# Seven products for one more down projection, keys and values kept in device memory, and waits by tile

## The chip, the cores and the metric

The kernel runs on one core of one Trainium2 chip. The core has five engines that work side by side, each through its own list of instructions in order: TensorE (PE in the profile, its weight loads PEld), VectorE (DVE), ScalarE (ACT), GpSimd (POOL) and SyncE (SP, which here only issues DMAs). DMAs are issued from the lists of SP, ACT and POOL and run on 16 DMA engines. The metric is the time of one execution on the device in microseconds (us), as the median of several runs; lower is better.

## What is computed

The reference is one step of a small two-layer decoder over 520 tokens: a prompt of 512 and 8 sample sequences with one token each. Every layer is half a SwiGLU feed-forward, a mixer, and another half feed-forward. Layer 0 mixes by causal pooling, layer 1 by sliding-window attention (window 128, 16 heads, 4 key/value heads) with keys and values that are projected once between the layers.

```python
def _swiglu(x, wg, wu, wd):
    return (jax.nn.silu(x @ wg) * (x @ wu)) @ wd      # D_MODEL 1024, D_FF 2816

for l in range(2):
    if l == 1:
        kv = _rmsnorm(x, kv_norm_g) @ w_kv            # shared keys (rotated) and values
        ...
    x = x + 0.5 * _swiglu(_rmsnorm(x, norm_g[l, 0]), w_gate[l, 0], w_up[l, 0], w_down[l, 0])
    x = x + (pool mixer of layer 0, or attention of layer 1)(_rmsnorm(x, norm_g[l, 1]))
    x = x + 0.5 * _swiglu(_rmsnorm(x, norm_g[l, 2]), w_gate[l, 1], w_up[l, 1], w_down[l, 1])
y = _rmsnorm(x, final_norm_g)
```

Beside `y` the step returns the last pooling inputs and the last window of keys and values, all in float32. There are four half feed-forwards ("half layers" 0 to 3); the change is about number 2, the first of layer 1.

## The kernel before

All activations stand transposed in on-chip memory: `x` is 8 tiles of 128 features by 520 tokens. Each float32 operand is split into a high and a low part that the matmul takes at full rate (`split`, line 315: ACT makes the high part, L319 and L322; DVE the low one, L320 and L323). A product of two operands is then three matmuls (`terms`: high by high, and the two mixed ones). A matmul has a weight block of 128x128 as the stationary operand and 260 tokens, half of the 520, as the moving one.

**Weights.** `Weights` (line 127) loads weights in chunks of 1 MB into three `raw` buffers (SP queue, L334), and splits them piece by piece into `wh` (ACT, L260) and `wl` (DVE, L261), up to five pieces ahead of PE (line 330). PE takes pieces in order with `W.get`.

**Feed-forward.** `ffn` (line 794) goes through the 22 hidden tiles of D_FF in three parts of 8, 8 and 6 (`PARTS`). In each part it makes the hidden tiles (gate, up, silu, product) and then adds the part's down projection onto `x`. The first `NPL` tiles of a half layer are plain (`mm`, L535), the others use Strassen's seven products in Winograd's form (`strassen_tile`, line 684; `product`, L563): weights and tokens are cut into 2 by 2 blocks, and 7 block products take the place of 8. The weights' sums are made by two accumulating DMAs from the POOL queue (L191, L192) and two DVE additions (L197, L201), the tokens' sums by DVE.

**Down projection.** It is plain too, save for the parts in `SEVEN` (line 33): the middle part of half layers 0, 1 and 3. There `HiddenSums` (line 586) makes the blocks and sums of the hidden tiles while they are produced, in the tiles `ph` and `pl` among others, and `strassen_down` (line 718) makes two of the eight output tiles at a time from 7 products. The plain one makes an output tile from 8 hidden tiles times 3 matmuls times 2 token halves and adds it to `x` (L823, L824).

**Keys and values.** Between half layers 1 and 2 the keys `kT` and the values `vtok` are made and stay in a pool `kvp` of their own until attention: `outputs` (line 1216) turns them and writes the window outputs from the POOL queue, `attention_prep` (line 1242) runs during the last down projection of half layer 2; it loads the old keys `kc` (L1247), puts the new ones into their first row (L1248) and splits `kT` and `vtok` into the operands of attention (`tl`). In attention every third softmax tile `sm` takes the place of `kT` in `kvp` (line 1363), the other two are in the pool `at`.

**What sets the order.** The kernel is traced into a scheduler that gives each engine its order of instructions by simulated times; what is marked with `later` or `seq` stays in the order of the program. The steps of attention follow the hand-written `PLAN` (line 60) and so does PE there. Memory comes from pools that are opened and closed one after another over the same addresses; as written, the first tile of a pool waits for the users of the pool that had its bytes.

Of the kernel before, what the change touches and what calls it, by code (L numbers as in the profile page):

```python
# [29 lines left out]

FIRST = 264
NPL = (4, 3, 2, 3)
SEVEN = {(0, 1), (1, 1), (3, 1)}
HD = 64
NB = SP // P
WINS = (2, 4, 8, 16)
# [244 lines left out]
def yoco_step(ctx, tc, ins, outs):  # L281
# [43 lines left out]
    def later(ins):  # L325

        return tc.keep_in_program_order(ins)
# [527 lines left out]
                by_parts(hs)  # L855

    def ff_pool():
        return tc.tile_pool(name="ff", bufs=2)

    def deferred(n, tmp, tag, tags, lst, w=TOK, hold=False):  # L860

# [166 lines left out]
        after = deferred(1, tmp, "g", XX, mov1, TW, True)  # L1028
        ffn(0, tmp, mov0, start_hooks(tmp, 0, tt, 2), tt, HH, after, pool_prep(), first, hold=True)

    with tc.tile_pool(name="pm", bufs=2) as pm:
        for k in range(KT):
            split(tuple(z[:, TOK:TW] for z in mov1[k]), sts[:, k, :])

# [109 lines left out]
        ffn(1, tmp, mov2, start_hooks(tmp, 2, tt, 2), tt, HH, deferred(N_KV, tmp, "g", XX, movk))  # L1144


    kvs = ExitStack()
    kvp = kvs.enter_context(tc.tile_pool(name="kvp", bufs=1))
    kT2 = kvp.tile([P, 2, TOK], F32, tag="kT", name="kT")
    kT = [kT2[:, g, :] for g in range(2)]  # L1150
    vtok = kvp.tile([P, NB, 256], F32, name="vtok")
    knew = kvp.tile([NS, 256], F32, name="knew")
    vnew = kvp.tile([NS, 256], F32, name="vnew")
    swap = [i + 8 if i < 8 else i - 8 if i < 16 else i for i in range(32)]

    def rope(out, banks, cosr, sinr, pool, tags):
# [11 lines left out]
    with ff_pool() as tmp:  # L1168

        s4 = sinks.rearrange("p (g i b e) -> p g i b e", g=2, i=4, b=4)  # L1170
        sr = sraw.rearrange("p (g e i) -> p g i e", g=2, e=2)
        for b in range(4):
            for g in range(2):
                V.tensor_copy(s4[:, g, :, b, :], sr[:, g])
        V.tensor_scalar(nsinks, sinks, -1.0, None, op0=ALU.mult)
        V.tensor_scalar(sink_s[:, 1:2], sink_s[:, 0:1], -1.0, None, op0=ALU.mult)
        cs = rawp.tile([P, 2, TOK], F32, tag="raw", name="cs")
        nc.scalar.dma_start(cs.rearrange("p a t -> p (a t)"), consts[:, C_COS : C_COS + 2 * TOK])

        def kv_pass(after):  # L1180
            banks = [duo() for _ in range(2)]
            for k0 in (0, 4):
                ws = [W.get(), W.get()]
                W.prefetch()
                for k in range(k0, k0 + 4):
                    for w, bk in zip(ws, banks):
                        mm(w, k - k0, movk[k], bk, k == 0, k == KT - 1)
                    after(k)
            return banks

        def during_k(k):
            if k == 1:
                rstd_tok()
            if k == 3:
                rstd_all()

        mov3, tt = [], {}
        steps = sums(tmp, 3, tt)

        def during_v(k):  # L1200
            mov3.append(pair(HH, [P, TOK]))
            split(mov3[k], x[k], gcol(3, k))
            if k >= 4:
                next(steps)

        kb = kv_pass(during_k)
        for i in range(2):
            V.tensor_tensor(cs[:, i, :], cs[:, i, :], R, op=ALU.mult)
        for g in range(2):
            rope(kT[g], kb[g], cs[:, 0, :], cs[:, 1, :], tmp, ("g", "t"))  # L1210
        vb = kv_pass(during_v)
        vT = [tmp.tile([P, TOK], F32, tag="g", name="vT") for g in range(2)]
        for g in range(2):
            V.tensor_tensor(halves(vT[g]), vb[g][:, :, :H], halves(R), op=ALU.mult)

        def outputs():
            win = tmp.tile([P, 256], F32, tag="t", name="win")
            pk = ps()
            for g in range(2):
                T.transpose(pk[:, g * P : (g + 1) * P], kT[g][:, 384:512], ident)  # L1220
                T.transpose(pk[:NS, 256 + g * P : 256 + (g + 1) * P], kT[g][:, SP:], ident)
            S.copy(win, pk[:, :256])
            S.copy(knew, pk[:NS, 256:512])
            nc.gpsimd.dma_start(k_win_p[0].rearrange("s g d -> s (g d)"), win)
            nc.gpsimd.dma_start(k_win_s[:, 127].rearrange("b g d -> b (g d)"), knew)
            for b2 in range(2):
                pv = ps()
                for b in (2 * b2, 2 * b2 + 1):
                    for g in range(2):
                        o = (b % 2) * 256 + g * P  # L1230
                        T.transpose(pv[:, o : o + P], vT[g][:, b * P : (b + 1) * P], ident)
                S.copy(vtok[:, 2 * b2 : 2 * b2 + 2, :], pv.rearrange("p (b c) -> p b c", b=2))  # L1232
            nc.gpsimd.dma_start(v_win_p[0].rearrange("s g d -> s (g d)"), vtok[:, 3, :])
            pvs = ps()
            for g in range(2):
                T.transpose(pvs[:NS, g * P : (g + 1) * P], vT[g][:, SP:], ident)
            S.copy(vnew, pvs[:NS, :256])
            nc.gpsimd.dma_start(v_win_s[:, 127].rearrange("b g d -> b (g d)"), vnew)

        kc, kk, vv = [], [], []  # L1240

        def attention_prep():


            for i in range(4):
                kc.append(splp.tile([P, 2, 256], F32, tag="S", name="kc", bufs=4))
                later(nc.sync.dma_start(kc[i], cache_k[2 * i : 2 * i + 2].rearrange("b s g d -> s b (g d)")))  # L1247
                nc.gpsimd.dma_start(kc[i][0:1], knew[2 * i : 2 * i + 2, :])  # L1248
            yield
            for i in range(4):  # L1250
                z = pair(("tl", "tl"), [P, SP])
                if i < 2:
                    kk.append(z)
                    split(z, kT[i][:, :SP])
                else:
                    vv.append(tuple(a.rearrange("p (b c) -> p b c", b=2) for a in z))
                    split(vv[-1], vtok[:, 2 * i - 4 : 2 * i - 2, :])
                if i:
                    yield
            for i in range(4):  # L1260
                pk = ps()
                for j in range(4):
                    T.transpose(pk[:, j * P : (j + 1) * P], kc[i][:, j // 2, (j % 2) * P : (j % 2 + 1) * P], ident)
                S.copy(kc[i].rearrange("p b c -> p (b c)"), pk)
                yield

        step = lambda: next(steps, None)
        hooks = [step, outputs] + [step] * 4
        ffn(2, tmp, mov3, hooks, tt, XX, deferred(4, tmp, "g", HH, mov4), attention_prep())


    mov5, mov6 = [], []
    with tc.tile_pool(name="at", bufs=2) as at:
        cst = at.tile([P, 512], F32, name="cst", bufs=1)
        nc.scalar.dma_start(cst, consts[:, C_MASK : C_MASK + 512])
        csq = at.tile([P, 2, TOK], F32, name="csq", bufs=1)
# [59 lines left out]
        class Unit:  # L1336
# [22 lines left out]
            def softmax(self):  # L1359

                c0 = self.t * 8 + self.h * 4
                nm, self.den = (at.tile([P, 4], F32, tag=n, name=n) for n in ("nm", "den"))
                pool = at if (2 * self.t + self.h) % 3 < 2 else kvp
                sm = pool.tile([P, 2, TOK], F32, tag="sm" if pool is at else "kT", name="sm")
                sm = sm.rearrange("p b (e c) -> p (b e) c", e=2)
                seq(V.tensor_copy(sm[:, :, 256], nsinks[:, c0 : c0 + 4]))
                self.sms = []
                for i in range(4):
                    bi, e = i // 2, i % 2
                    b = self.bs[bi]  # L1370
                    n = 256 if b else P
                    mk = C_MASK + 256 if b else C_MASK
                    self.sms.append(sm[:, i, 256 - n :])
                    seq(
                        V.tensor_tensor_reduce(  # L1375
                            out=sm[:, i, 256 - n : 256],
                            in0=self.pe[e][:, bi * 256 : bi * 256 + n],
                            in1=cst[:, mk : mk + n],
                            op0=ALU.add,
                            op1=ALU.min,  # L1380
                            scale=nr8[:, b : b + 1],
                            scalar=nsinks[:, c0 + i : c0 + i + 1],
                            accum_out=nm[:, i : i + 1],
                        )
                    )
                for i in range(4):
                    z = sm[:, i, 256 - (256 if self.bs[i // 2] else P) : 257]
                    seq(
                        S.activation(
                            z, z, AF.Exp, scale=-1.0, bias=nm[:, i : i + 1], accum_out=self.den[:, i : i + 1]  # L1390
                        )
                    )
# [179 lines left out]
        def load_values():  # L1572
            vc.append(rawp.tile([P, NS, 256], F32, tag="raw", name="vc"))
            later(nc.sync.dma_start(vc[0], cache_v.rearrange("b s g d -> s b (g d)")))
            nc.gpsimd.dma_start(vc[0][0:1], vnew)

        def w_load(n):
            W.load(o_chunk + n)
# [35 lines left out]
        after_o = deferred(5, at, "rp0", XX, mov6)  # L1614
        for m in range(KT):
            o_part(m, 4, after=after_o)

    kvs.close()

    with ff_pool() as tmp:  # L1620
        tt = {}
# [239 lines left out]
```

## Time and profile before

| | us |
|---|---|
| median of 3 runs (lowest, highest) | 1674.66 (1671.61, 1676.63) |
| the profiled execution, its own time | 1678.03 |
| its span, first to last instruction | 1676.2 |
| what lies around the span | 1.83 |

The profile has one execution. A busy share is the time in which an engine works, over the span. The views used below are the page with its chain of waits (which engine the end of the program hung on, followed backwards), the busy time of every engine in chosen stretches, the list of waits of an engine, the groups of instructions, and the timeline. In a row of the stretches stand the length, then for each engine the busy time and the number of instructions, the granted clock of TensorE, the busy share of the DMA engines and GB/s. In a timeline row stand start, duration, engine, line, operation, output<-inputs, and in brackets the idle time before it with what ended it. The mean granted clock of the run is 0.991.

### The profile page before, as it was taken

To read this page: it belongs to the slowest core of one execution; us is meant where nothing else is said; L and a number is where in the kernel's file an instruction comes from. 1 tells how busy PE (TensorE), PEld (TensorE's weight loads), DVE (VectorE), ACT (ScalarE), POOL (GpSimd) and SP (SyncE) were. 2 spreads that over 40 slices of the span, in tenths; PEclk is the share of its full clock that TensorE was granted. 3 is DMA by queue.
4 is the path that set the end of the run, shared out by engine and by line. 5 is a ranking of instruction groups with operands and counts; after the bars stand their busy time and mean duration, and the time that the engine had idled before them with its cause. 6 is when DMAs were issued, how large, how long until landed. Compare 5 with 4: busy or idle time off the path is not lost.

```text
span 1676.2 us, 34643 instructions
## 1 busy us (share of the span) xinstructions
PE 1644.5 (98%) x13626; PEld 1632.1 (97%) x13626; DVE 1307.3 (78%) x2532; ACT 920.7 (55%) x1867; POOL 187.0 (11%) x248
## 2 busy tenths in 40 slices
PE   9999999999999999999999999999889999999997
PEld 9999999999999999999999999999889999999997
DVE  6866999887875999888775875886776785799876
ACT  5743655665652664655552642655775663465555
POOL 0101111000101111101101101101210100111100
PEclk9999999999999999999999999999979999999999
DMA  8545778753555778645645855644122545577851
GB/s 223 132 133 125 174 184 177 187 167 88 110 151 127 178 170 198 149 130 133 148 143 127 173 147 127 155 140 105 42 51 76 133 114 156 130 180 174 178 134 52
DMA packets 337199, 235.42 MB, mean 140 GB/s; under 512 B 10878, under 2 KB 309606, under 8 KB 336996
## 3 DMA queue, kind: packets, MB, share of 16 engines
q1 hardware_dynamic: 306814, 181.00, 38.4%
q0 software_dynamic: 26464, 47.12, 17.6%
q10 hardware_dynamic: 3758, 5.09, 1.0%
q8 instruction: 107, 1.75, 0.4%
q14 instruction: 56, 0.46, 0.1%
HBM read 183.45 MB, written 5.04 MB: 112 GB/s over the span
## 4 chain that ended last, share of the span: by engine, by line
PE 89%; DVE 5%; DMA 2%; ACT 2%; issue 2%; POOL 0%; ACTq 0%; DVEq 0%; POOLq 0%
PE ps L563 50%; PE ps L535 33%; DMA S<-raw 1%; DVE wl L261 1%; PE ps L1445 1%; PE ps L1077 1%; DMA pr<-in_bands_dram 0%; DVE sm L1375 0%; PE ps L1052 0%; PE ps L1538 0%; PE ps L1735 0%; DVE xl L320 0%; PE ps L1414 0%; ACT wh L260 0%; PE ps L1357 0%
## 5 line engine op out<-in xcount | busy, mean ns | idle before, releaser
L260 ACT ACTIVATE wh<-raw 128x512 fp32r<-128x512 f32 (+1 forms) x754 | 449.4, 620 | 425.8 <-PE ps L535 232.1
L261 DVE TENSOR_TENSOR wl<-raw,wh 128x512 fp32r<-128x512 f32 (+1 forms) x754 | 495.1, 675 | 153.1 <-ACT wh L260 150.6
L563 PE MATMUL ps<-th,wh 128*128 128x260 f32 x1216 | 344.0, 283 | 1.7 <-ACT sa L701 0.9
L563 PE MATMUL ps<-tl,wh 128*128 128x260 f32 x1216 | 342.4, 282 | 0.0
L563 PE MATMUL ps<-th,wl 128*128 128x260 f32 x1216 | 341.0, 282 | 0.2 <-DVE wl L261 0.2
L563 PEld LDWEIGHTS ps<-th,wh 128*128 128x128 f32 x1216 | 228.5, 188 | 3.6 <-ACT sa L701 1.4
L563 PEld LDWEIGHTS ps<-tl,wh 128*128 128x128 f32 x1216 | 229.0, 188 | 0.0
L563 PEld LDWEIGHTS ps<-th,wl 128*128 128x128 f32 x1216 | 227.9, 188 | 0.4 <-DVE wl L261 0.4
L192 POOL DMA_DIRECT2D raw<-raw x88 | 75.8, 862 | 1177.2 <-DVE wl L261 452.3
L563 PE MATMUL ps<-xh,wh 128*128 128x260 f32 x720 | 203.1, 283 | 0.7 <-ACT sb L698 0.7
L563 PE MATMUL ps<-xl,wh 128*128 128x260 f32 x720 | 202.3, 282 | 0.0
L563 PE MATMUL ps<-xh,wl 128*128 128x260 f32 x720 | 200.9, 282 | 0.0
L535 PE MATMUL ps<-hh,wh 128*128 128x260 f32 x956 | 193.7, 284 | 0.6 <-ACT vtok L1232 0.6
L535 PE MATMUL ps<-hl,wh 128*128 128x260 f32 x956 | 193.4, 283 | 0.0
L535 PE MATMUL ps<-hh,wl 128*128 128x260 f32 x956 | 192.3, 283 | 0.0
L535 PE MATMUL ps<-xl,wh 128*128 128x260 f32 x736 | 149.7, 284 | 0.3 <-DVE xl L951 0.3
L535 PE MATMUL ps<-xh,wh 128*128 128x260 f32 x736 | 149.0, 285 | 0.0
L535 PEld LDWEIGHTS ps<-hh,wh 128*128 128x128 f32 x956 | 147.1, 189 | 1.5 <-ACT vtok L1232 0.9
L535 PE MATMUL ps<-xh,wl 128*128 128x260 f32 x736 | 148.0, 283 | 0.0
L535 PEld LDWEIGHTS ps<-hl,wh 128*128 128x128 f32 x956 | 147.9, 189 | 0.0
L535 PEld LDWEIGHTS ps<-hh,wl 128*128 128x128 f32 x956 | 147.6, 189 | 0.0
L563 PEld LDWEIGHTS ps<-xh,wh 128*128 128x128 f32 x720 | 135.4, 188 | 1.3 <-ACT sb L698 1.3
(325 smaller groups left out, 3369.6 us busy)
## 6 DMA issues: line engine op xcount, KB each, us to landing
raw<-in_ffn_w_gate_dram SPq DMA_DIRECT2D x87, 512.0 KB, 4.2
raw<-in_ffn_w_up_dram SPq DMA_DIRECT2D x87, 512.0 KB, 6.5
raw<-raw POOLq DMA_DIRECT2D x88, 256.0 KB, 3.4
S<-raw POOLq DMA_DIRECT2D x88, 256.0 KB, 4.5
raw<-in_ffn_w_down_dram SPq DMA_DIRECT2D x20, 1024.0 KB, 4.9
S<-in_ffn_w_up_dram SPq DMA_DIRECT2D x76, 256.0 KB, 6.0
raw<-in_ffn_w_down_dram SPq DMA_DIRECT2D x48, 256.0 KB, 4.0
raw<-in_ffn_w_down_dram SPq DMA_DIRECT2D x16, 768.0 KB, 4.3
```

The lines of the kernel that those rows point to most:

```text
L192: G.dma_start(blk(raw, 2, 1), blk(raw, 1, 1), accum_op=ALU.add)
L260: pin(nc.scalar.activation(dh, src, AF.Copy))
L261: pin(nc.vector.tensor_tensor(dl, src, dh.bitcast(F32), op=ALU.subtract))
L535: ins = T.matmul(banks[:, hf, :H], a[:, kk, :], hcols(b, hf), start=(first and i == 0), stop=(last and i == 2),)
L563: T.matmul(bank[:, :H], a[:, kk, :], b, start=(not more and kk == 0 and i == 0), stop=(kk == 3 and i == 2), skip_group_check=more,)
L1077: T.matmul(po[:, half * 256 : half * 256 + 256], z[:, tau, c], b, start=(i == 0), stop=(i == len(lst) - 1),)
L1445: T.matmul(po[:, bi * 256 : (bi + 1) * 256], a, p_[:, kc_], start=(n == 0), stop=(n == 3 * len(kts) - 1),)
```

## The change

The middle part of half layer 2 joins `SEVEN`. For its sums the pool of the half layer needs room, and so `kvp` leaves on-chip memory: `kT`, `vtok`, `knew` and `vnew` become short-lived tiles that share the places of later feed-forward tiles, their contents are written to device memory right after they are made (six more DMAs on the POOL queue), and `attention_prep` loads keys and values back into tiles `kept` (four DMAs on the SP queue, behind those of `kc`) and splits these. The rows for `kc` and for the old values come from device memory too. Attention's third `sm` buffer moves into its pool. Four pools (`ff`, `pm`, `at`) are opened with `reuse_waits="tile"`: a tile that takes over bytes of a closed pool waits for the users of those bytes alone.

```diff
-SEVEN = {(0, 1), (1, 1), (3, 1)}
+SEVEN = {(0, 1), (1, 1), (2, 1), (3, 1)}
...
-        return tc.tile_pool(name="ff", bufs=2)
+        return tc.tile_pool(name="ff", bufs=2, reuse_waits="tile")
...
-    with tc.tile_pool(name="pm", bufs=2) as pm:
+    with tc.tile_pool(name="pm", bufs=2, reuse_waits="tile") as pm:
...
-    kvs = ExitStack()
-    kvp = kvs.enter_context(tc.tile_pool(name="kvp", bufs=1))
-    kT2 = kvp.tile([P, 2, TOK], F32, tag="kT", name="kT")
-    kT = [kT2[:, g, :] for g in range(2)]
-    vtok = kvp.tile([P, NB, 256], F32, name="vtok")
-    knew = kvp.tile([NS, 256], F32, name="knew")
-    vnew = kvp.tile([NS, 256], F32, name="vnew")
+    kvp = ctx.enter_context(tc.tile_pool(name="kvp", bufs=1, space=bass.MemoryType.DRAM))
+    kT_kept = [kvp.tile([P, SP], F32, name=f"kT_kept{g}") for g in range(2)]
+    v_kept = [kvp.tile([P, 2, 256], F32, name=f"v_kept{b}") for b in range(2)]
+    k_new, v_new = (kvp.tile([NS, 256], F32, name=n) for n in ("k_new", "v_new"))
...
+        kT = [tmp.tile([P, TOK], F32, tag="ph", name="kT", bufs=3) for g in range(2)]
...
+            knew = tmp.tile([NS, 256], F32, tag="sb", name="knew", bufs=2)
+            vnew = tmp.tile([NS, 256], F32, tag="sb", name="vnew", bufs=2)
             S.copy(knew, pk[:NS, 256:512])
             nc.gpsimd.dma_start(k_win_p[0].rearrange("s g d -> s (g d)"), win)
             nc.gpsimd.dma_start(k_win_s[:, 127].rearrange("b g d -> b (g d)"), knew)
+            nc.gpsimd.dma_start(k_new, knew)
+            for g in range(2):
+                nc.gpsimd.dma_start(kT_kept[g], kT[g][:, :SP])
...
-                S.copy(vtok[:, 2 * b2 : 2 * b2 + 2, :], pv.rearrange("p (b c) -> p b c", b=2))
-            nc.gpsimd.dma_start(v_win_p[0].rearrange("s g d -> s (g d)"), vtok[:, 3, :])
+                vtok = tmp.tile([P, 2, 256], F32, tag="pl", name="vtok", bufs=3)
+                S.copy(vtok, pv.rearrange("p (b c) -> p b c", b=2))
+                nc.gpsimd.dma_start(v_kept[b2], vtok)
+            nc.gpsimd.dma_start(v_win_p[0].rearrange("s g d -> s (g d)"), vtok[:, 1, :])
...
             nc.gpsimd.dma_start(v_win_s[:, 127].rearrange("b g d -> b (g d)"), vnew)
+            nc.gpsimd.dma_start(v_new, vnew)
...
-                nc.gpsimd.dma_start(kc[i][0:1], knew[2 * i : 2 * i + 2, :])
+                nc.gpsimd.dma_start(kc[i][0:1], k_new[2 * i : 2 * i + 2, :])
+            kept = []
+            for i in range(4):
+                kept.append(tmp.tile([P, SP], F32, tag="ph" if i < 2 else "pl", name="kept", bufs=3))
+                src = kT_kept[i] if i < 2 else v_kept[i - 2].rearrange("p b c -> p (b c)")
+                later(nc.sync.dma_start(kept[i], src))
...
-                    split(z, kT[i][:, :SP])
+                    split(z, kept[i])
...
-                    split(vv[-1], vtok[:, 2 * i - 4 : 2 * i - 2, :])
+                    split(vv[-1], kept[i].rearrange("p (b c) -> p b c", b=2))
...
-    with tc.tile_pool(name="at", bufs=2) as at:
+    with tc.tile_pool(name="at", bufs=2, reuse_waits="tile") as at:
...
-                pool = at if (2 * self.t + self.h) % 3 < 2 else kvp
-                sm = pool.tile([P, 2, TOK], F32, tag="sm" if pool is at else "kT", name="sm")
+                sm = at.tile([P, 2, TOK], F32, tag="sm", name="sm", bufs=3)
...
-            nc.gpsimd.dma_start(vc[0][0:1], vnew)
+            nc.gpsimd.dma_start(vc[0][0:1], v_new)
...
-    kvs.close()
```

## The prediction

> **What bounds the kernel now.** I read the page first, then the stage that the change alters beside its three sisters, then the waits. From the top of the page and its chain of waits:
>
> ```profile
> span 1676.2 us, 34643 instructions
> PE 1644.5 (98%) x13626; PEld 1632.1 (97%) x13626; DVE 1307.3 (78%) x2532; ACT 920.7 (55%) x1867; POOL 187.0 (11%) x248
> ...
> PE 89%; DVE 5%; DMA 2%; ACT 2%; issue 2%; POOL 0%; ACTq 0%; DVEq 0%; POOLq 0%
> ```
>
> TensorE is busy for 98% of the span, and 89% of the chain that ended last is TensorE's own work. So a matmul taken away shortens the program by its issue time, as long as the engine behind it keeps up: VectorE with 78% on average is the one to watch. Averages hide the stage, so here are the same stretches of the four half layers, from the first block product (L563) of the middle part's hidden tiles to the last one of the third part's:
>
> ```profile
> core 0: us, PE busy (x) PEld busy (x) DVE busy (x) ACT busy (x) POOL busy (x), PEclk, DMA share, GB/s
> 149.40:327.40 178.00, 176.58 (x1467) 175.78 (x1466) 158.96 (x289) 104.11 (x211) 26.02 (x30) 1.00 0.74 171
> 536.60:713.50 176.90, 176.32 (x1467) 175.53 (x1466) 158.96 (x288) 104.00 (x210) 26.00 (x30) 1.00 0.71 166
> 911.40:1092.70 181.30, 181.30 (x1515) 181.30 (x1515) 136.92 (x232) 93.22 (x178) 19.19 (x22) 1.00 0.61 144
> 1442.10:1618.70 176.60, 176.31 (x1467) 175.66 (x1467) 158.96 (x288) 103.82 (x210) 26.08 (x30) 1.00 0.73 166
> ```
>
> The ends of two of them on TensorE, half layers 1 and 2:
>
> ```profile
> 536.62 0.28 PE L563 MATMUL ps<-xh,wh 128*128 128x260 f32 x1
> ...
> 713.34 0.28 PE L563 MATMUL ps<-th,wl 128*128 128x260 f32 x1
> ```
>
> ```profile
> 911.46 0.28 PE L563 MATMUL ps<-hh,wh 128*128 128x260 f32 x1
> ...
> 1092.51 0.28 PE L563 MATMUL ps<-th,wl 128*128 128x260 f32 x1
> ```
>
> Half layer 2 (third row) has the plain middle down projection: 1515 matmuls without a gap. Half layers 0, 1 and 3 already have seven products there: 1467 matmuls, and a little less TensorE work than time. After the change the order of TensorE's instructions in half layer 2 is the one that half layers 1 and 3 have now, around and in this stretch; so they are the price list.
>
> **The middle down projection.** It goes from 384 to 336 matmuls, 48 fewer, which is also 1515 - 1467. One costs 181.30 / 1515 = 0.1197 us where nothing waits, so 48 are 5.74 us. Not all of it arrives: half layer 1 is only 181.3 - 176.9 = 4.4 us shorter, half layer 3 4.7, half layer 0 3.3. What is given back (1.34, 1.04 and 2.44 us) are short waits for the sums that the seven products need; in the list of waits of half layers 0 and 1 together (a row: total, times, longest) and then of half layer 3, they read as follows, while half layer 2 has none at all:
>
> ```profile
> PE ps L563 <- ACT sa L701: 0.9, 1, 0.9
> ...
> PE ps L563 <- DVE sb L708: 0.5, 2, 0.3
> PE ps L563 <- ACT sb L698: 0.5, 2, 0.2
> ```
>
> ```profile
> PE ps L563 <- ACT sb L698: 0.2, 1, 0.2
> ```
>
> The `sa` wait is half layer 0's alone. I take the mean of the two with the same order, 1.2 us, and 1.04 to 2.44 as bounds: -5.74 + 1.2 = **-4.55 us**. VectorE's share of the stretch goes from 136.92 / 181.30 = 76% to 158.96 / 176.90 = 90%, below the bound. ScalarE's 104 us and GpSimd's 26 us of 177 stay far from it, the eight added accumulating DMAs among them:
>
> ```profile
> L191 POOL DMA_DIRECT2D S<-raw x88 | 89.8, 1020 | 39.5 <-DMA S<-in_ffn_w_down_dram 18.3 <-DMA S<-in_ffn_w_up_dram 11.0 <-DVE xl L320 2.7
> ```
>
> At 1.02 us each they are 8.2 us more of GpSimd's list, which its three sisters carry already.
>
> **Keys and values out.** Six more writes go into GpSimd's list, beside four that are there, and the small result tiles now take the place of `sb`:
>
> ```profile
> 793.01 1.24 POOL L1224 DMA_DIRECT2D out_dram<-win  x1
> ...
> 799.46 0.83 POOL L1238 DMA_DIRECT2D out_dram<-vnew  x1
> 817.53 0.89 POOL L192 DMA_DIRECT2D raw<-raw  x1 [17.23 <-DVE wl L261]
> ```
>
> ```profile
> 808.43 0.35 ACT L698 COPY sb<-ps 128x260 f32<-128x260 f32 x1
> ```
>
> ```profile
> kc<-in_cache_k_win_dram SPq DMA_DIRECT2D x4, 256.0 KB, 6.8
> ...
> out_dram<-win POOLq DMA_DIRECT2D x1, 128.0 KB, 6.6
> out_dram<-vtok POOLq DMA_DIRECT2D x1, 128.0 KB, 3.6
> ```
>
> Queued behind them on GpSimd is the next weight sum; before it the engine is idle for 17.23 us, until 817.53, anyway, and six issues of about 1 us fit. The first `sb` of the next half layer (808.43) must wait for the writes of `knew` and `vnew`: issued until about 801, landed 3.6 to 6.6 us after (the last rows), so at 808 at the latest. Cost 0; if that cover is gone, ScalarE is held at its copy, with TensorE behind it, for the microsecond or two that a write is late.
>
> **Keys and values back.** Four more loads of 256 KB follow `kc` on SP's list, and the operands `tl` are split from them, no longer in advance:
>
> ```profile
> 1101.30 1.35 ACT L319 ACTIVATE tl<-vtok 128x512 fp32r<-128x512 f32 x2 [1.40 <-PE ps L563]
> ```
>
> ```profile
> 1102.91 0.68 DVE L320 TENSOR_TENSOR tl<-vtok,tl 128x512 fp32r<-128x512 f32 x1
> ```
>
> ```profile
> 1106.29 2.20 SPq L1247 DMA_DIRECT2D kc<-in_cache_k_win_dram  x4
> ```
>
> ```profile
> 1112.35 0.55 POOL L1248 DMA_DIRECT2D kc<-knew  x1 [40.09 <-DMA kc<-in_cache_k_win_dram]
> ```
>
> ```profile
> 1108.00:1112.00 4.00, 4.00 (x36) 4.00 (x35) 4.00 (x8) 2.92 (x7) 0.00 (x0) 1.00 1.11 327
> 1112.00:1116.00 4.00, 4.00 (x36) 4.00 (x35) 4.00 (x8) 2.06 (x5) 2.12 (x4) 1.00 0.46 136
> 1116.00:1124.00 8.00, 8.00 (x70) 8.00 (x69) 7.62 (x14) 5.53 (x11) 0.00 (x0) 1.00 0.57 158
> ```
>
> The four `kc` loads land within 1112.35 - 1106.29 = 6.1 us at 327 GB/s. 1 MB more at that rate takes 1.05 MB / 327 GB/s = 3.2 us, so the last `kept` is there at about 1115.5, and the splits move from around 1101 to around 1113 to 1118. There VectorE has no free time (4.00 of 4.00, then 7.62 of 8.00), and four splits of 0.68 us add 2.7 us to its list; ScalarE may stand still before the split for a few us with the next weight pieces behind it. The cover is the weight pieces split ahead, five of 18 matmuls: 5 x 18 x 0.1197 = 10.8 us. I take 0, and keep 0 to +2.7 as bounds: the splits have left an earlier place on VectorE, so it starts this stretch less far behind. The values were written some 300 us earlier, so no load waits for a write. The one write here whose landing I can read took 3.6 us, and any round trip is hidden by that distance. [...]
>
> **Waits by tile.** What ends earlier is the idle time of ScalarE ahead of the first `xa` of two half layers' sums:
>
> ```profile
> DVE acc L483: 1.5, 2
> ```
>
> 1.5 us in two waits, and TensorE is not behind them directly. I take 0, bounds -1.5 to 0; other waits by tile only move to earlier users.
>
> **Attention's order.** The `sm` buffers and the short splits shift ScalarE's and VectorE's order a little in attention; a copy of `oT` comes ahead of some exponentials. TensorE is held there by it now:
>
> ```profile
> 1220.08 0.73 ACT L1464 COPY oT<-ps 64x256 f32<-64x256 f32 x2
> ...
> 1220.87 0.58 PE L1445 MATMUL ps<-xh,tl 128*128 128x256 f32 x1 [1.56 <-ACT oT L1464]
> ```
>
> ```profile
> 1197.00:1238.00 41.00, 30.51 (x262) 27.45 (x262) 36.70 (x125) 37.21 (x112) 9.38 (x18) 0.96 0.15 33
> ```
>
> That wait of 1.56 us can go, but ScalarE works 37.21 of 41 us and VectorE 36.70, so most of it comes back at the next softmax. I take a quarter, -0.4, with -1.6 (all kept) and +2.0 (the exponentials that are now later hold TensorE instead, a little more than the wait that left) as bounds.
>
> **Sum.** -4.55 + 0 + 0 + 0 - 0.4 = -4.95 us: the span goes from 1676.2 to 1671.3. The profiled execution took 1678.03 us, 3.37 above the median of the runs shown, so I apply the difference to the median: 1674.66 - 4.95 = **1669.7 us**. A measurement of this kernel can tell 0.3%, here 5.0 us, so the forecast stands on that line.
>
> **Rivals.**
> - *Attention and the pools give more.* The 1.56 us wait goes for good: -4.55 - 1.6, or with the 1.5 us of the `xa` waits instead, -4.55 - 0.4 - 1.5: 1668.2 to 1668.5. For it: TensorE is idle 10 of 41 us there. Against: both other engines are nearly full.
> - *VectorE becomes the bound of the stage.* Half layer 2 gives back what half layer 0 does, 2.44 us, because VectorE carries the 90% and then has the splits of keys and values ahead of it: -3.3 us, 1671.4. For it: the full rows at 1108 to 1124. Against: half layers 1 and 3 with the same order.
> - *Slower: ScalarE is held by the loads that come back.* A split waits in order on ScalarE, the weight pieces wait behind it, and TensorE behind those. If the four loads come one after another at the 6.8 us of `kc`, the last is there after 27.2 us; less the 10.8 us of cover this is +16.4 - 4.95, or 1686.1. It decides from a hold of 10.8 + 4.95 = 15.8 us on. Against: four such loads did land together within 6.1 us.
> - *The change does not do what it says*: with the plain order kept the time would be 1674.7. The list of TensorE's instructions, 48 shorter, leaves no room for this.
>
> **How the numbers follow.** The forecast 0.62, half of it on either side of the 5.0 us (0.31 and 0.31); attention and pools 0.17, faster; VectorE as bound 0.14, within 0.3%; slower 0.07. So faster 0.48, within 0.3% 0.45, slower 0.07. The range 1666.5 to 1674.0 takes in the bounds on the gain's side (-4.7 - 1.6 - 1.5 = -7.8, 1666.9) and on the other -3.3 with the 2.7 us of the moved splits (-0.6, 1674.0); it leaves out the slower case.
>
> **What would show it.** Right: the stretch of half layer 2 lasts 176.6 to 176.9 us with 1467 matmuls and VectorE at 159 us; the waits for `sb` (L698, L708 in the old lines) of 0.2 to 0.3 us appear in it; no wait of TensorE in the last down projection of half layer 2, ScalarE idle under 3 us before the split of `kept`; the 1.56 us wait for `oT` gone; a span near 1671.3. Wrong: a stretch above 178 us, TensorE waiting for weight pieces where `kept` is split, writes of keys and values still in flight when `sb` is taken, or more TensorE idle time in attention than the 10 us of 41 now.

## The result

| | kernel before | changed kernel |
|---|---|---|
| median of the executions, us (lowest, highest; count) | 1675.64 (1669.57, 1678.99; 8) | 1667.15 (1662.59, 1671.43; 8) |
| ratio, 95% interval | 1 | 0.9955 (0.9934 to 0.9976) |
| span of the profiled execution, us | 1676.2 | 1661.8 |
| granted clock of it | 0.991 | 0.995 |

The change gains 0.45%, between 0.24% and 0.66%. The forecast was 4.95 us and 1669.7, with a range of 1666.5 to 1674.0. The two profiled executions differ by 14.4 us, the medians by 8.5, so the first thing to settle is which part of those 14.4 us belongs to the change.

The page of the changed kernel, for the lines shown of before:

```profile
span 1661.8 us, 34718 instructions
...
PE 1633.8 (98%) x13578; PEld 1621.9 (98%) x13578; DVE 1329.6 (80%) x2589; ACT 931.6 (56%) x1900; POOL 196.5 (12%) x262
...
PE 92%; ACT 3%; DVE 2%; issue 1%; DMA 1%; POOL 0%; ACTq 0%; DVEq 0%; POOLq 0%
```

TensorE sets the pace as before. Busy time by stage, same columns as in the prediction: half layer 2's stretch in the changed kernel, from its first to its last block product.

```profile
911.25:1087.09 175.84, 175.60 (x1466) 175.18 (x1464) 159.23 (x288) 104.11 (x210) 26.05 (x30) 1.00 0.75 167
```

It lasted 1092.51 - 911.46 = 181.05 us before (the two end rows in the prediction). So 5.2 us went here, with VectorE at the 159 us that were forecast. Its list of TensorE's waits has one line:

```profile
PE ps L563 <- ACT sb L698: 0.2, 1, 0.2
```

Then attention, cut into its first 60 us and the rest, from the last matmul of the query projection ahead of the scores of unit 3 to the first matmul of the output projection behind the turn of unit 14 (its 16 units are numbered 0 to 15; a unit's turn is the transposition of its softmax). The kernel before, then the changed kernel:

```profile
1178.13:1238.13 60.00, 49.51 (x439) 45.58 (x438) 49.77 (x175) 49.93 (x151) 12.50 (x23) 0.97 0.17 45
1238.13:1267.90 29.77, 29.77 (x197) 29.02 (x196) 18.44 (x65) 15.34 (x50) 3.18 (x4) 0.72 0.21 47
```

```profile
1171.25:1231.25 60.00, 52.65 (x444) 48.70 (x443) 48.96 (x173) 50.08 (x151) 12.09 (x23) 0.91 0.17 43
1231.25:1252.71 21.46, 21.46 (x192) 20.87 (x191) 17.71 (x63) 14.68 (x49) 3.10 (x4) 1.00 0.29 64
```

Attention takes 89.8 us in the one and 81.5 in the other, and the 8.3 us lie in the second part, where TensorE is busy without a gap in both: 197 matmuls in 29.77 us at a clock of 0.72, against 192 in 21.46 us at 1.00. That is a slower clock, not more work. Whether the change brought the better clock can't be read from one execution of each. The next difference lies between half layer 2's stretch and this one: the last down projection of half layer 2 and most of attention's query projection, from the first plain matmul behind the last block product on. It takes 1178.13 - 1102.29 = 75.8 us before and 1171.25 - 1096.75 = 74.5 us after. Below and in the expectations this is the stretch "up to attention".

### The profile page after: what moved, and what is told of

Read it like the earlier page. It is cut to its first block, busy times and chain, and to the rows that moved or that the text cites. A ratio compares the mean times of both kernels' runs of the same rounds, so it can differ in the third digit from the quotient of the medians.

```text
span 1661.8 us, 34718 instructions
## 1 busy us (share of the span) xinstructions
PE 1633.8 (98%) x13578; PEld 1621.9 (98%) x13578; DVE 1329.6 (80%) x2589; ACT 931.6 (56%) x1900; POOL 196.5 (12%) x262
## 4 chain that ended last, share of the span: by engine, by line
PE 92%; ACT 3%; DVE 2%; issue 1%; DMA 1%; POOL 0%; ACTq 0%; DVEq 0%; POOLq 0%
PE ps L563 55%; PE ps L535 31%; DMA pr<-in_bands_dram 1%; PE ps L1077 1%; PE ps L1455 1%; ACT sm L1399 1%; PE ps L1052 0%; PE ps L1424 0%; ACT xh L319 0%; PE ps L494 0%; PE ps L1743 0%; DVE wl L261 0%; PE ps L1368 0%; ACT wh L260 0%; PE ps L932 0%
## 5 line engine op out<-in xcount | busy, mean ns | idle before, releaser
L261 DVE TENSOR_TENSOR wl<-raw,wh 128x512 fp32r<-128x512 f32 (+1 forms) x762 | 501.0, 678 | 136.4 <-ACT wh L260 133.7
L563 PE MATMUL ps<-xh,wh 128*128 128x260 f32 x784 | 220.9, 283 | 0.7 <-ACT sb L698 0.7
L563 PE MATMUL ps<-xl,wh 128*128 128x260 f32 x784 | 220.3, 282 | 0.0
L563 PE MATMUL ps<-xh,wl 128*128 128x260 f32 x784 | 218.7, 282 | 0.0
L192 POOL DMA_DIRECT2D raw<-raw x92 | 79.3, 862 | 1148.1 <-DVE wl L261 421.1
L535 PE MATMUL ps<-hl,wh 128*128 128x260 f32 x956 | 193.2, 282 | 0.0
L563 PEld LDWEIGHTS ps<-xh,wh 128*128 128x128 f32 x784 | 147.3, 188 | 1.3 <-ACT sb L698 1.3
L563 PEld LDWEIGHTS ps<-xl,wh 128*128 128x128 f32 x784 | 147.5, 188 | 0.0
L563 PEld LDWEIGHTS ps<-xh,wl 128*128 128x128 f32 x784 | 146.9, 189 | 0.0
L563 PE MATMUL ps<-hl,wh 128*128 128x260 f32 x448 | 125.8, 282 | 0.0
```

What stands on the lines that cost most here:

```text
L192: G.dma_start(blk(raw, 2, 1), blk(raw, 1, 1), accum_op=ALU.add)
L261: pin(nc.vector.tensor_tensor(dl, src, dh.bitcast(F32), op=ALU.subtract))
L535: ins = T.matmul(banks[:, hf, :H], a[:, kk, :], hcols(b, hf), start=(first and i == 0), stop=(last and i == 2),)
L563: T.matmul(bank[:, :H], a[:, kk, :], b, start=(not more and kk == 0 and i == 0), stop=(kk == 3 and i == 2), skip_group_check=more,)
```

## The experiments

Theory 1 was the prediction's: the stage gives the gain, the rest of the change next to nothing, and attention's 8.3 us are clock that differs from one execution to the next. Its rivals put part of the gain into attention's new order, into the waits by tile, or let the detour of keys and values cost something.

**after_again**: the changed kernel, no edit.

> The changed kernel once more, for a second profile on another chip. All theories: ratio 0.9955, between 0.993 and 0.998. Theory 1 (what the profile showed beyond the 5.2 us of the stage, 8.3 us less in attention, is half-clock time of TensorE that falls differently in each execution): half layer 2's stretch again 175.5 to 176.5 us, but attention (from the end of the last down projection's matmuls to the next half layer) differs from the first profile's 81.5 us by several us, and the granted clock with it. Theory 2 (attention's new order saves a fixed 2 to 8 us): attention again within 1 us of 81.5.

Ratio 0.9952 (0.9935 to 0.9969). Its profile has the stretch at 1085.77 - 909.68 = 176.09 us and this attention:

```profile
1169.94:1229.94 60.00, 51.81 (x448) 47.73 (x446) 49.36 (x175) 50.30 (x152) 12.10 (x23) 0.94 0.17 43
1229.94:1257.27 27.33, 27.33 (x189) 26.58 (x188) 17.43 (x61) 14.57 (x48) 3.11 (x4) 0.75 0.22 51
```

The same program, 5.9 us longer in attention, again at 0.75 in the gapless part. So the clock there is not fixed by the program, and theory 2 (attention within 1 us of 81.5 us again) is out.

**plain_2**: the seven products of half layer 2 taken back.

```diff
-SEVEN = {(0, 1), (1, 1), (2, 1), (3, 1)}
+SEVEN = {(0, 1), (1, 1), (3, 1)}
```

> The changed kernel with half layer 2's middle down projection plain again (48 matmuls back); keys and values through device memory, waits by tile and attention's buffers stay. Theory 1: half layer 2's stretch is back at 181.0 to 181.3 us, the rest of the change is worth nothing: time 5 us above the changed kernel, ratio to before 0.9985 to 1.001. Theory 2: the rest of the change gains by itself 2 to 4 us: ratio 0.9975 or less, and attention shorter than before's 89.8 us at an equal clock. Theory 3 (the detour of keys and values costs something that the stage's gain hid): ratio above 1.001, with waits of TensorE in the last down projection of half layer 2.

Ratio 0.9974 (0.9961 to 0.9988). That is the ratio of theory 2 (0.9975 or less), while the interval reaches into that of theory 1 (0.9985 or more). Part of it is the clock: none of these 12 executions had a granted clock of 0.991 or less, against 12 of 35 of the kernel before beside them. At a clock of 0.994 or more the median spans are 1666.4 and 1668.0 us, which is 1.6 us for the rest of the change. The stretch is back at 181.04 us, without a wait of TensorE in it or in the stretch up to attention:

```profile
909.59:1090.63 181.04, 181.04 (x1513) 181.04 (x1512) 136.87 (x231) 93.51 (x177) 19.20 (x22) 1.00 0.60 145
```

So the 5 us of the stage are the seven products. Theory 3, a hidden cost of the detour, is out.

**no_tile** and **tile_only**: waits by tile taken away from the changed kernel, and given to the kernel before. Every engine's order stays the same, only the waits differ. The edit names three kinds of pools; `ff` is opened four times, so they are six pools.

```diff
-        return tc.tile_pool(name="ff", bufs=2, reuse_waits="tile")
+        return tc.tile_pool(name="ff", bufs=2)
...
-    with tc.tile_pool(name="pm", bufs=2, reuse_waits="tile") as pm:
+    with tc.tile_pool(name="pm", bufs=2) as pm:
...
-    with tc.tile_pool(name="at", bufs=2, reuse_waits="tile") as at:
+    with tc.tile_pool(name="at", bufs=2) as at:
```

> The changed kernel with all pools waiting for the whole pool before, as in the kernel before; the order of every engine is the same. Theory 1: same time as the changed kernel within 1.5 us (ratio 0.9955, 0.993 to 0.998), with the two waits of ScalarE ahead of the first xa (1.5 us in total) back. Theory 4 (the waits by tile are where the gain beyond the stage is from): 2 to 3 us slower than the changed kernel, ratio 0.997 or more.

> The kernel before with waits by tile in the three kinds of pools and nothing else; the order of every engine is the same. Theory 1: ratio 1.000 (0.998 to 1.002). Theory 4: 0.998 or less.

Ratios 0.9961 (0.9946 to 0.9976) and 0.9989 (0.9972 to 1.0006). Both ratios lie in the ranges of theory 1, and the intervals reach into those of theory 4, so they decide nothing. The profiles do. With whole-pool waits TensorE has a wait in the stretch up to attention, at the query projection's per-token norm, that the waits by tile don't have; the kernel before and no_tile:

```profile
PE ps L508 <- DVE r_tok L503: 1.2, 1, 1.2
```

```profile
PE ps L508 <- DVE r_tok L503: 0.5, 1, 0.5
```

and the stretch up to attention is 75.8 and 75.3 us, against 74.5 (changed kernel) and 74.4 (tile_only). ScalarE's timeline ahead of it says why. Before, then tile_only:

```profile
1136.60 0.62 ACT L479 ACTIVATE sq<-x 128x520 f32<-128x520 f32 x1
1138.13 0.34 ACTq L1275 DMA_DIRECT2D cst<-in_consts_dram  x1
1138.50 1.42 ACTq L1277 DMA_DIRECT2D csq<-in_consts_dram  x1
1139.95 1.28 ACT L1475 ACT_TABLE_LOAD   x1 [2.73 <-issue]
```

```profile
1134.26 0.33 ACTq L1275 DMA_DIRECT2D cst<-in_consts_dram  x1
1134.88 0.62 ACT L479 ACTIVATE sq<-x 128x520 f32<-128x520 f32 x1
1136.41 0.34 ACTq L1277 DMA_DIRECT2D csq<-in_consts_dram  x1
1136.78 1.28 ACT L1475 ACT_TABLE_LOAD   x1 [1.27 <-DVE acc L483]
```

Two loads of constants for attention (`cst`, `csq`) are issued from ScalarE's list into attention's pool. With whole-pool waits they stand until the last user of the half layer's pool is done, and behind them in order stand the table load for the exponential, the weight splits and so the norm that L508 waits for. By tile, `cst` is issued ahead of the last square (L479), and the table load starts 1.27 us after ScalarE's last work instead of 2.73. `csq` is still held there: it starts 0.91 us after the end of the last square, as `cst` does in the kernel before. Of the 1.46 us between the two rows 0.37 is the issue of `cst`, and 1.08 is that the issue of `csq` took 0.34 us instead of 1.42, for a reason that no run shows. With keys and values in device memory the same comparison is cleaner. Here is no_tile, then the changed kernel, where both loads are issued ahead of the last square and the table load follows it at once:

```profile
1133.30 0.45 ACTq L1288 DMA_DIRECT2D csq<-in_consts_dram  x1
1133.79 1.28 ACT L1485 ACT_TABLE_LOAD   x1 [1.76 <-DVE acc L483]
```

```profile
1131.22 0.45 ACTq L1288 DMA_DIRECT2D csq<-in_consts_dram  x1
1131.48 0.62 ACT L479 ACTIVATE sq<-x 128x520 f32<-128x520 f32 x1
1132.12 1.28 ACT L1485 ACT_TABLE_LOAD   x1
```

**tile_at**: attention's pool alone by tile, on the kernel before.

```diff
-    with tc.tile_pool(name="at", bufs=2) as at:
+    with tc.tile_pool(name="at", bufs=2, reuse_waits="tile") as at:
```

> The kernel before with waits by tile in attention's pool alone. Theory 5 (what waits by tile save is the hold of ScalarE's two loads of constants, cst and csq, by the whole pool of the half layer before, with the exponential's table load queued behind them): as with all three kinds of pools, no wait of TensorE at the per-token norm (L508) and the stretch of matmuls of the last down projection up to attention 74.4 us instead of 75.8; ratio 0.998 to 1.000. Rival (another of the pools does it): 75.3 us or more.

The stretch is 1175.18 - 1100.79 = 74.4 us and there is no wait at L508: it is this pool. The ratio, 0.9990 (0.9973 to 1.0007), is that of tile_only. The two waits of ScalarE ahead of the first `xa` (1.5 us in total), which the prediction named, are still there in tile_at and gone in tile_only; at a clock of 0.994 or more the two have median spans of 1666.1 and 1666.3 us, so those waits are worth nothing that shows.

**detour_only**: the edits of plain_2 and no_tile together, which leaves keys and values through device memory, with attention's third `sm` buffer in its own pool and the order that follows from both, as the difference to the kernel before.

```diff
-SEVEN = {(0, 1), (1, 1), (2, 1), (3, 1)}
+SEVEN = {(0, 1), (1, 1), (3, 1)}
...
-    with tc.tile_pool(name="at", bufs=2, reuse_waits="tile") as at:
+    with tc.tile_pool(name="at", bufs=2) as at:
```

> The kernel before with the detour of keys and values through device memory alone: plain middle down projection in half layer 2, whole-pool waits. Theory (revised: stage and waits by tile give the gain at an equal clock, the detour nothing): executions at a granted clock of 0.994 or more take 1667 to 1668.5 us as the kernel before (1667.6), the stretch of the last down projection up to attention is 75.2 to 75.9 us again with a wait at L508; ratio 0.998 to 1.001, below 1 only if fewer executions fall to a clock of 0.991 or less (before: 25 of 64). Rival (the detour's new order in attention saves 1.5 us or more at an equal clock): 1666 us or less at 0.994 or more, ratio 0.998 or less.

Ratio 1.0000 (0.9985 to 1.0015): the detour, its new order in attention included, is worth nothing within 2.5 us either way, and 0.3 us at a clock of 0.994 or more (1667.3 and 1667.6). The L508 wait is there (0.6 us), and the stretch up to attention takes 75.3 us.

**kept_twice**: each load of keys and values issued twice.

```diff
                 later(nc.sync.dma_start(kept[i], src))
+                later(nc.sync.dma_start(kept[i], src))
```

> The changed kernel with each of the four loads of keys and values issued twice into the same tile, so that the splits wait for both. Theory 1 (the cover is weight pieces split ahead, 10.8 us, of which 1.45 us is used): ScalarE is held 4 to 9 us ahead of the first split and TensorE still has no wait there; ratio as the changed kernel, 0.994 to 0.998. Rival (the cover is nearly used up): TensorE waits 2 us or more for weight pieces in the last down projection, ratio 0.997 or more.

Ratio 0.9958 (0.9941 to 0.9975). The waits of ScalarE for these loads, changed kernel and kept_twice (total, times, longest):

```profile
ACT tl L319 <- DMA kept<-kT_kept: 1.4, 1, 1.4
```

```profile
ACT tl L319 <- DMA kept<-v_kept: 2.9, 2, 2.3
...
ACT tl L319 <- DMA kept<-kT_kept: 1.7, 2, 1.1
```

ScalarE is held 4.6 us instead of 1.4, in four waits of at most 2.3 us, and not 4 to 9 us ahead of the first split as expected. TensorE has no wait for a weight piece in either; what shows is 0.5 us at L508, and where that comes from was not followed up. So the cover was not used up by these waits; a hold near its 10.8 us was not tried.

**before_fill, after_fill, after_fill_2**: filler matmuls (ones by ones, into a bank that the next step overwrites; the kernel before has a few already) where TensorE stands still right before attention's gapless part, five in the kernel before and in the changed kernel, and two in the changed one. The profile of before has 1.53 us of idle time there and puts it down to "issue" (L1414); no run shows that it is a softmax that ends it. A filler earlier in that attention took 0.24 us for 128 columns of unsplit float32 (from 1215.53 to the next matmul at 1215.77), where a matmul on split operands took 0.1197 us for 260.

```diff
-FILL_T = (0, 0, 0, 0, 0, 0, 2, 1, 0, 0, 1, 0, 0, 0, 0, 0)
+FILL_T = (0, 0, 0, 0, 0, 0, 2, 1, 0, 0, 1, 5, 0, 0, 0, 0)
```

```diff
-FILL_T = (0, 0, 0, 0, 0, 0, 2, 1, 0, 0, 1, 0, 0, 0, 0, 0)
+FILL_T = (0, 0, 0, 0, 0, 0, 2, 1, 0, 0, 1, 2, 0, 0, 0, 0)
```

> The kernel before with five filler matmuls on TensorE (1.2 us at full clock) ahead of the turn of attention's unit 11, where TensorE waits 1.53 us for the softmax right before the dense stretch that ends attention. Theory 1 (most of attention's 8.3 us is half-clock time in that dense stretch, and the clock falls because of the gaps ahead of it): the dense stretch runs at full clock, attention takes 81 to 83 us instead of 89.8, ratio to before 0.996 to 0.999. Rival (the clock falls by earlier gaps, or by chance alone): attention 84 us or more with 0.50 in the stretch, ratio 0.999 to 1.002.

> The changed kernel with the same five filler matmuls. Theory 1: the clock no longer falls in the dense stretch in some executions: attention 81 to 82 us, ratio to before 0.992 to 0.995, the best of all kernels here. Rival (chance, or earlier gaps): ratio as the changed kernel, 0.995 to 0.997.

> The changed kernel with two filler matmuls (0.5 us) ahead of the turn of unit 11 instead of five, which kept all 23 timed executions above 0.991 but cost 1 to 2 us of TensorE's time. If two are enough for the clock: no execution at 0.991 or less, 1662 to 1663 us at 0.994 or more, ratio 0.993 to 0.9955. Rival (two are too few, low clocks are as frequent as without): 3 or more of 12 at 0.991 or less, ratio 0.995 to 0.997.

Ratios 0.9992 (0.9976 to 1.0007), 0.9965 (0.9951 to 0.9979) and 0.9973 (0.9960 to 0.9985). The first two lie in the ranges of the rivals, the third just above the rival's. In the profile of before_fill attention takes 84.1 us, between theory 1 and the rival's half clock; its part behind the first 60 us is

```profile
1237.73:1261.85 24.12, 24.12 (x203) 23.55 (x202) 18.02 (x63) 14.80 (x49) 3.18 (x4) 0.93 0.24 58
```

at a clock of 0.93 instead of the 0.72 of the kernel before. The profiles of tile_only and tile_at have a clock of 0.50 there for 15 us too (from 1235.00 and from 1234.78 on). Each timed execution has its own span and granted clock, so the kernels can also be compared where the clock is the same:

| | executions | with a clock of 0.991 or less | median span of those | median span at 0.994 or more |
|---|---|---|---|---|
| before | 84 | 29 | 1674.2 | 1667.6 |
| detour_only | 12 | 3 | 1672.2 | 1667.3 |
| tile_only and tile_at | 24 | 8 | 1673.4 | 1666.1 |
| plain_2 | 12 | 0 | | 1666.4 |
| no_tile | 12 | 3 | 1668.6 | 1663.7 |
| changed kernel | 20 | 7 | 1667.4 | 1662.0 |
| kept_twice | 7 | 0 | | 1664.0 |
| before_fill | 12 | 0 | | 1668.5 |
| after_fill | 11 | 0 | | 1663.9 |
| after_fill_2 | 10 | 0 | | 1663.8 |

The last column rests on 4 to 11 executions in every row but the first, and the rows come from different chips, so differences of a microsecond are at its limit: kept_twice, the changed kernel but for four more loads, stands 2.0 us above it, of which its profile shows 0.9 in the stretch up to attention (75.4 instead of 74.5).

With fillers no execution out of 33 had a clock of 0.991 or less, against 36 of 104 of the two kernels without. For the kernel before (0 of 12 in before_fill, against 13 of 29 beside it) that speaks for the gaps ahead of the gapless part as what brings the low clock on. It is not shown for the changed kernel: plain_2 and kept_twice have no execution at 0.991 or less either, 0 of 19, without any added filler, so another cause that differs between kernels is open. At 0.994 or more the fillers cost about 1 to 2 us, about what they save on average. The expectation for after_fill, the best of all kernels, did not come true, nor did that of 1662 to 1663 us for after_fill_2, though its clock stayed up as expected; no kernel here is clearly faster than the changed one.

## Why the prediction was right, and where it was off

- *The middle down projection, -4.55 us.* Right in mechanism, a little small in size. The stretch is 4.9 to 5.2 us shorter in the profiles (181.05 to 176.2 at most in no_tile, 1087.00 - 910.81, and 175.84 at least). The term that was mis-sized is what the stage gives back: it was taken as the mean of half layers 1 and 3, 1.2 us, and measured 0.5 to 0.9 (5.74 less 5.2 or 4.86). That these are waits for the sums is only partly so: in the changed kernel TensorE is idle for 175.84 - 175.60 = 0.24 us of the stretch, and half layer 3, which gives back 1.04, for 176.60 - 176.31 = 0.29; the rest stands in the rows as busy time. Half layer 1's own price was that of one execution: its stretch lasts 713.34 - 536.62 = 176.72 us in the profile of before, and 713.15 - 537.13 = 176.02 in that of the changed kernel, where nothing in it is changed. At an equal clock the whole program shows 1666.4 - 1662.0 = 4.4 us for it with waits by tile, 1667.3 - 1663.7 = 3.6 without.
- *Keys and values, 0.* Right, out and back, within what detour_only can tell (1.0000, 0.9985 to 1.0015). ScalarE was held 1.45 us before the first split, under the 3 us that were named, as this row of the changed kernel shows, and the round trip hid in the time between write and read:

```profile
1109.94 1.93 ACT L319 ACTIVATE tl<-kept 128x512 fp32r<-128x512 f32 x3 [1.45 <-DMA kept<-kT_kept]
```

The writes took longer to land than the 3.6 us that the prediction took for the only readable write (the row of `win` beside it has 6.6), which changes nothing over some 300 us; the last column is the median from issue to landing:

```profile
kT_kept<-kT POOLq DMA_DIRECT2D x2, 256.0 KB, 5.3
v_kept<-vtok POOLq DMA_DIRECT2D x2, 256.0 KB, 6.8
```

- *Waits by tile, 0, bounds -1.5 to 0.* The 0 was wrong, and the bound of -1.5 held about, for another reason. The prediction counted as idle time that ends earlier only that ahead of `xa`, which was indeed worth nothing (tile_at beside tile_only), and called the other waits moves to earlier users. The wait that mattered was a DMA issue in ScalarE's list, held by the pool (in the kernel before together with the long issue of `csq` behind it). Before, it showed only as idle time put down to "issue" (2.73 us ahead of the table load) and as TensorE's 1.2 us at L508. Without waits by tile the stretch up to attention is 0.8 to 1.4 us longer (75.3 and 75.8 against 74.5 and 74.4), and the program 1.2 to 1.7 us at an equal clock (1667.6 less 1666.1 or 1666.4, and 1663.7 less 1662.0).
- *Attention's order, -0.4.* Nothing fixed was gained that detour_only could show, so this quarter did not come. The 1.56 us wait for `oT` did go, and waits of the same kind stand at other places, as the changed kernel's list in attention shows. The profile pair's 8.3 us are the clock: at 0.53 for 17.87 us (last section) the kernel before lost an estimated 17.87 x 0.47 = 8.4 us there.

```profile
PE ps L529 <- ACT oT L1474: 1.7, 2, 1.4
PE ps L1512 <- ACT oT L1474: 1.4, 1, 1.4
...
PE ps L1424 <- ACT oT L1474: 1.2, 1, 1.2
```

- *The sum.* By the runs: 4.4 for the stage, 1.2 for the waits, 0 for the detour, together 5.6 us at an equal clock (1667.6 - 1662.0; steps of one chain, which add up by construction). The other chain, by detour_only and no_tile, gives 0.3, 3.6 and 1.7. The medians measured 6.9 to 8.5 us (after_again: 1671.93 - 1665.08; the first comparison: 1675.64 - 1667.15). The share of low-clock executions was the same for both kernels, 7 of 20 and 29 of 84, and 5.6 us of span, or 5.3 of time with the 2.0 to 2.2 us that lie around the changed kernel's spans and 1.7 to 1.8 before, is in both intervals (4.0 to 11.1 us and 5.2 to 10.9), so the rest of the difference is not resolved. That the forecast of 4.95 comes near 5.6 is partly luck: the -0.4 for attention did not come, and the 1.2 for the waits was not foreseen. So is the hit in time: the median of the kernel before moved between 1669.9 and 1675.6 us from one comparison to the next, and 1667.15 stands 0.65 us inside the range.
- *Rivals.* "Attention and the pools give more" held by half: the pools, though not by the `xa` waits that it named, and not attention. VectorE did not become the bound (159.23 of 175.84 us, 0.2 us of waits of TensorE), and ScalarE's hold of 1.45 us stayed far from the 15.8 us from which the slower case would have decided.

From the last block product of half layer 3 to the end of the span the changed kernel takes 1661.8 - 1603.5 = 58.3 us and the one before 1676.2 - 1618.5 = 57.7. These 0.6 us were not followed up.

## What to carry to other kernels

When a price is taken from sister stages, one profiled execution of each has an error of its own, here 0.7 us of a gain of 5 (half layer 1 in two profiles). In the kernel before, the issues of two DMAs stood in ScalarE's list like instructions, 0.34 and 1.42 us long, with the table load behind them: when pools are opened over old bytes, look for DMAs into the new pool on busy engines, and for what is queued behind them. And before a difference between two profiles is explained, compare the granted clock stage by stage, and the spans at equal clocks: 8 of these 14 us were not the change's.

## What the hardware showed beyond expectation

In the kernel before TensorE ran without a gap in the second part of attention and yet at a clock of 0.53 for 17.87 us, after gaps of 1.77 and 1.53 us in the 8 us ahead of it (two rows of its timeline, then two stretches):

```profile
1232.32 0.46 PE L529 MATMUL ps<-ones 128*128 128x128 f32 x2 [1.77 <-DVE smx L1519]
...
1237.71 1.75 PE L1414 MATMUL ps<-ident,sm 128*128 128x128 f32 x8 [1.53 <-issue]
```

```profile
1238.13:1256.00 17.87, 17.87 (x93) 17.42 (x92) 10.40 (x43) 9.15 (x33) 3.18 (x4) 0.53 0.26 57
1256.00:1267.90 11.90, 11.90 (x106) 11.60 (x105) 8.04 (x22) 6.19 (x18) 0.00 (x0) 1.00 0.12 33
```

93 matmuls in 17.87 us, then 106 in 11.90. How long the clock stays down differs between executions of one program (a clock of 1.00 and of 0.75 in the second part of attention in the two profiles of the changed kernel). Of the spread of the kernel before, 1665.0 to 1677.6 us, 6.6 us lie between the medians at a low and at a high clock (1674.2 and 1667.6). What sets how long it stays down is open.
